# Two-layer decoder trunk: the mixer's output projection sums the squares of six first-half tiles, and the FFN loads the other two first

## The chip, the cores and the metric

The kernel runs on one core of one Trainium2 chip. The metric is the device time of one execution in microseconds (us); of several runs the median is given. The engines are called as in the profile: PE is TensorE, PEld its weight loads, DVE is VectorE, ACT is ScalarE, POOL is GpSimd, and SP is SyncE, which here issues the DMAs.

## What is computed

The reference is a decoder trunk of two layers on 1024 positions of width 1024, all in float32. Layer 0 mixes positions by a gated delta rule, layer 1 by stick-breaking attention. What matters here is the step from the mixer's output to the FFN, the same in both layers:

```
h = h + o.reshape(b_, s_, WIDTH) @ w_out          # output projection and residual
h = h + swiglu(rms_norm(h, ln_ffn[i]), ffn_w_in[i], ffn_w_out[i])

def rms_norm(x, g):
    y = x * lax.rsqrt(jnp.mean(x * x, axis=-1, keepdims=True) + EPS)
    return y * g
```

So the FFN's input needs, for each position, the mean over 1024 features of the squared result of the output projection.

## The kernel before

**Layout.** The activations lie transposed: features on partitions, positions along the free dimension. A half is 512 positions; the 1024 features are eight tiles of 128 partitions, so a half of the residual stream is eight tiles of 128x512. Matmul operands are kept as a rounded high part and a low part (hi and lo), and a product of two such operands takes three matmuls (`mm3`, line 351). One tile of a projection is therefore 8 x 3 = 24 matmuls into one PSUM bank.

**Order of the work.** The program is written as generators that a planner (`Flow`, lines 83 to 259) interleaves while the program is built. The main generator feeds the matmuls of the large products; others are spawned with a rank (lower goes first) and are resumed when the planner's clock says that what they last issued is ready. The clock is an estimate with a cost for each operation; it advances with TensorE's matmuls, and a DMA's landing is estimated with one ring of 360 GB/s (lines 202 to 204). The result is a fixed order of instructions on each engine's queue; an engine works through its queue in order and waits on semaphores where an input isn't there yet. Tiles come from pools; those with one tag share a number of buffers, and a new tile waits until a buffer of its tag is free.

**The stages round the change.** `out_first` (line 1266) makes the first half of the output projection, tile by tile. For each tile f its helper `put` loads the residual tile into a buffer (`ca` in layer 0, `xt` in layer 1), adds the projection's bank on DVE, and writes the sum to memory (`h1D`). It runs at the end of the mixer: in layer 0 from `gdn` (line 665), in layer 1 from `attention` (line 1790), where the first tiles are interleaved with the last attention steps. The mixer's pools are then closed, and `tail` (line 1302) opens those of the FFN.

`tail` makes the second half of the output projection, and its helper `put` adds each bank to a residual tile that stays in SBUF. Beside that, `load(0)` brings the first half back from `h1D` into eight tiles `u`, and for each half a generator `norm` runs at rank 1: for tile after tile `sumsq` (line 532) squares it on ACT and adds it to an accumulator `acc` on DVE (the first square goes into the accumulator directly); then `rstd` (line 544) sums the accumulator over the partitions by four matmuls with one column of ones each (tile `st`), `root` (line 552) takes the mean plus a small constant on DVE and its power -1/2 on POOL, and `normed` (line 561) spreads the result over the partitions by four matmuls and multiplies and splits the eight tiles.

When both halves are normalized, `first` and `combine` (lines 1341 and 1422) build sums and differences of the four quarter blocks on DVE, operands of a fast scheme with seven products instead of eight; the FFN's first weight pair (`f_in`, names `fg` and `fu`) is multiplied plainly with the two halves, and the rest (`f_s`) with those combinations. The weights pass through two load buffers `raw`, are split on ACT (high part) and on DVE or POOL (low part), and sit in three slots `w` and one slot `e`.

The second half of layer 0's last normalization uses a small persistent tile `r1` (line 300): it is written near the end of layer 0's tail and read at the start of attention.

## Time and profile before

| What | Before |
|---|---|
| Median of 3 runs | 2774.21 us (2772.11 to 2776.08) |
| The profiled execution's own time | 2772.17 us |
| Its span | 2770.5 us |
| PE busy in the span | 2735.0 us (99%) |
| DVE, ACT, POOL busy | 1945.8, 1325.1, 868.4 us |
| Weight loads on PE | 2273.6 us (82%) |
| Data moved by DMA | 394.85 MB, mean 143 GB/s |
| Granted TensorE clock, mean | 0.998 |

The profile is of one execution on the chip. Its page gives busy time by engine, the chain of work that ended last, and groups of instructions; the trace behind it answers for any stretch of time with busy times, with instructions in order of time (start, duration, operation, output<-inputs, count, and in brackets the idle time of the engine before it with what ended it), and with who waited for whom. Nearly all instructions pass through one helper and so carry line 64 (L64); they are told apart by the names of their tiles.

### The profile page before, as it was taken

To read this page: it belongs to the slowest core of one execution; us is meant where nothing else is said; L and a number is where in the kernel's file an instruction comes from. 1 tells how busy PE (TensorE), PEld (TensorE's weight loads), DVE (VectorE), ACT (ScalarE), POOL (GpSimd) and SP (SyncE) were. 2 spreads that over 40 slices of the span, in tenths; PEclk is the share of its full clock that TensorE was granted. 3 is DMA by queue.
4 is the path that set the end of the run, shared out by engine and by line. 5 is a ranking of instruction groups with operands and counts; after the bars stand their busy time and mean duration, and the time that the engine had idled before them with its cause. 6 is when DMAs were issued, how large, how long until landed. Compare 5 with 4: busy or idle time off the path is not lost.

```text
span 2770.5 us, 37795 instructions
## 1 busy us (share of the span) xinstructions
PE 2735.0 (99%) x13203; PEld 2273.6 (82%) x13203; DVE 1945.8 (70%) x3727; ACT 1325.1 (48%) x2701; POOL 868.4 (31%) x750
## 2 busy tenths in 40 slices
PE   9999999999999999999999999999999999999999
PEld 8788888888778888888888888888878888888787
DVE  7687888873875655477867778887696555557783
ACT  6655555543444434222335778877443333322241
POOL 0111111100166666444201222221036666634410
PEclk9999999999999999999999999999999999999999
DMA  4412222246434444577342111114514444477723
GB/s 147 144 59 77 73 77 75 74 151 234 159 107 152 164 153 148 222 313 305 124 137 100 47 58 54 54 58 149 209 61 160 150 153 142 156 288 282 279 82 125
DMA packets 165073, 394.85 MB, mean 143 GB/s; under 512 B 34001, under 2 KB 35345, under 8 KB 155409
## 3 DMA queue, kind: packets, MB, share of 16 engines
q1 hardware_dynamic: 164880, 392.43, 40.3%
q8 instruction: 104, 1.70, 0.3%
q14 instruction: 89, 0.72, 0.1%
HBM read 273.77 MB, written 118.59 MB: 142 GB/s over the span
## 4 chain that ended last, share of the span: by engine, by line
PE 88%; DVE 6%; ACT 2%; issue 2%; DMA 1%; POOL 0%; SPq 0%; ACTq 0%; POOLq 0%; DVEq 0%
PE dn L64 42%; PE mm L64 33%; PE tp L64 4%; PE z L64 3%; PE c L64 2%; PE o L64 2%; PE po L64 1%; DVE x L64 1%; PE rc L64 1%; PE st L64 1%; ACT junk L64 1%; PE r L64 1%; DVE y L64 1%; DVE v L64 0%; DVE acc L64 0%
## 5 line engine op out<-in xcount | busy, mean ns | idle before, releaser
L64 PE MATMUL mm<-x,whi 128*128 128x512 f32 x2592 | 860.1, 401 | 6.1 <-DVE x L64 5.8
L64 PE MATMUL dn<-x,whi 128*128 128x512 f32 x2032 | 628.7, 390 | 1.4 <-DVE v L64 0.9
L64 PEld LDWEIGHTS mm<-x,whi 128*128 128x128 f32 x2592 | 480.3, 189 | 94.7 <-DVE x L64 10.2
L64 PE MATMUL mm<-x,wlo 128*128 128x512 f32 x1296 | 518.7, 400 | 0.0
L64 POOL TENSOR_TENSOR wlo<-raw,whi 128x512 fp32r<-128x512 f32 x244 | 349.2, 1452 | 407.1 <-ACT whi L64 392.5
L64 ACT CAST whi<-raw 128x1024 fp32r<-128x1024 f32 x231 | 242.7, 1051 | 446.3 <-DVE raw L64 253.7
L64 PEld LDWEIGHTS dn<-x,whi 128*128 128x128 f32 x2032 | 381.4, 188 | 82.2 <-DVE x L64 2.1
L64 PE MATMUL dn<-x,wlo 128*128 128x512 f32 x1016 | 396.4, 390 | 0.0
L64 PEld LDWEIGHTS mm<-x,wlo 128*128 128x128 f32 x1296 | 244.8, 189 | 41.1 <-issue 0.3
L64 PE MATMUL dn<-hx,whi 128*128 128x512 f32 x896 | 276.9, 390 | 0.4 <-DVE hx L64 0.4
L64 PEld LDWEIGHTS dn<-x,wlo 128*128 128x128 f32 x1016 | 190.9, 188 | 39.2
L64 PEld LDWEIGHTS dn<-hx,whi 128*128 128x128 f32 x896 | 168.2, 188 | 36.3 <-DVE hx L64 1.3
L64 DVE TENSOR_TENSOR v<-v,dn 128x512 f32<-128x512 f32 x112 | 76.4, 686 | 170.4 <-PE dn L64 169.5
L64 DVE TENSOR_TENSOR tt<-u,tt 128x512 fp32r<-128x512 f32 x140 | 133.3, 952 | 80.7 <-ACT tt L64 80.7
L64 PE MATMUL dn<-hx,wlo 128*128 128x512 f32 x448 | 175.0, 391 | 3.4 <-POOL wlo L64 3.4
L64 DVE TENSOR_TENSOR wlo<-raw,whi 128x512 fp32r<-128x512 f32 x218 | 148.9, 694 | 27.2 <-ACT whi L64 26.6
L64 POOL TENSOR_TENSOR wlo<-sw,whi 128x512 fp32r<-128x512 f32 x102 | 144.8, 1437 | 0.0
L64 ACT CAST tt<-u 128x512 fp32r<-128x512 f32 x140 | 84.9, 620 | 123.0 <-DMA yD<-tt 101.6
L64 DVE TENSOR_TENSOR E<-E,dn 128x512 f32<-128x512 f32 x132 | 90.0, 684 | 70.6 <-PE dn L64 68.4
L64 PE MATMUL dn<-x,ehi 128*128 128x512 f32 x400 | 123.5, 390 | 2.3 <-ACT v L64 2.3
L64 POOL TENSOR_TENSOR rs<-ms,nhalf 128x4 f32<-128x4 f32 x11 | 12.0, 1087 | 338.7 <-DVE ms L64 338.7
L64 DVE SCALAR_TENSOR_TENSOR ca<-xe,conv,ca 128x512 f32<-128x512 f32 x144 | 106.2, 744 | 0.9 <-ACT ca L64 0.5
(381 smaller groups left out, 5092.4 us busy)
## 6 DMA issues: line engine op xcount, KB each, us to landing
yD<-tt SPq DMA_DIRECT2D x296, 256.0 KB, 2.5
x<-yD SPq DMA_DIRECT2D x58, 1024.0 KB, 11.4
raw<-f_s SPq DMA_DIRECT2D x84, 512.0 KB, 3.6
raw<-d_s SPq DMA_DIRECT2D x40, 512.0 KB, 5.1
raw<-w_in SPq DMA_DIRECT2D x33, 512.0 KB, 4.0
hx<-yD SPq DMA_DIRECT2D x16, 1024.0 KB, 13.9
x<-oD SPq DMA_DIRECT2D x26, 512.0 KB, 5.1
raw<-g_out SPq DMA_DIRECT2D x16, 512.0 KB, 4.7
```

The source lines that it names most:

```text
L64: r = issue(*args, **kw)
```

## The change

The squares of the first six of the first half's eight tiles are no longer taken in `tail` from the tiles that were loaded back. `out_first` spawns a generator `squares` for each of its first six tiles, at rank 2, as soon as the tile is added. The first square makes an accumulator, the others are added to it; behind the sixth, four matmuls with a column of ones sum it over the partitions, and DVE writes that sum times 1/1024 plus the small constant into the tile `r1`. Accumulator and squares use free buffers of the mixer's pools: tag `xe` in layer 0, `rw` in layer 1. In `tail`, `load(0)` brings tiles 6 and 7 first, the first half's `norm` squares and adds just these two, and `root` adds `r1` in place of the constant. The second half is as before. The mixer's end also waits until `r1` is marked.

```diff
-    def rstd(self, pool, acc, r):
+    def rstd(self, pool, acc, r, more=None):
...
-        yield from self.root(pool, st, r)
-
-    def root(self, pool, st, r):
+        yield from self.root(pool, st, r, more)
+
+    def root(self, pool, st, r, more=None):
         nc = self.nc
         ms = self.t(pool, "ms", (P, 4))
-        nc.vector.tensor_scalar(ms, st[:, :4], 1.0 / D, EPS, op0=ALU.mult, op1=ALU.add)
+        if more is None:
+            nc.vector.tensor_scalar(ms, st[:, :4], 1.0 / D, EPS, op0=ALU.mult, op1=ALU.add)
+        else:
+            nc.vector.scalar_tensor_tensor(ms, st[:, :4], 1.0 / D, more, op0=ALU.mult, op1=ALU.add)
...
-            yield from self.out_first(0, io["xT"], self.tmp)
-            yield lambda: all(e in flow.at for e in ("loaded00", "loaded01", ("put", 0)))
+            yield from self.out_first(0, io["xT"], self.tmp, lambda: self.g("xe", (P, HW + 3))[:, :HW])
+            yield lambda: all(e in flow.at for e in ("loaded00", "loaded01", ("put", 0), ("r1", 0)))
...
-    def out_first(self, layer, hsrc, tmp):
+    def out_first(self, layer, hsrc, tmp, room):
...
+        acc = []
+
+        def squares(xt):
+            if not acc:
+                acc.append(room())
+                yield from self.sumsq(None, acc[0], xt, True)
+            else:
+                acc.append(None)
+                yield from self.sumsq(room, acc[0], xt, False)
+            if len(acc) < NK - 2:
+                return
+            st = yield from self.bank()
+            for j in range(4):
+                self.mmul(st[:, j : j + 1], acc[0][:, j * P : (j + 1) * P], self.ones[:, :1])
+            yield
+            nc.vector.tensor_scalar(self.r1, st[:, :4], 1.0 / D, EPS, op0=ALU.mult, op1=ALU.add)
+            self.unbank(st)
+            flow.mark(("r1", layer))
...
             nc.sync.dma_start(self.h1D[layer][f][:, :HW], xt)
+            if f < NK - 2:
+                flow.spawn(squares(xt), 2)
             if f == NK - 1:
                 flow.mark(("put", layer))
...
             def load(hf):
-                for k in range(NK):
+                for k in range(NK) if hf else (6, 7, 0, 1, 2, 3, 4, 5):
...
             def norm(hf):
                 a = self.t(fp, "acc", bufs=2)
-                for k in range(NK):
+                ks = range(NK) if hf else (NK - 2, NK - 1)
+                for k in ks:
                     yield lambda: flow.done(("h1", layer, hf, k))
-                    yield from self.sumsq(lambda: self.t(fp, "tt", bufs=4), a, H1[hf, k], k == 0)
+                    yield from self.sumsq(lambda: self.t(fp, "tt", bufs=4), a, H1[hf, k], k == ks[0])
                 r = self.t(fp, "rs", (P, 4))
-                yield from self.rstd(fp, a, r)
+                yield from self.rstd(fp, a, r, None if hf else self.r1)
...
-            yield from self.out_first(1, self.hD, lambda: self.t(sp, "xt"))
-            yield lambda: all(e in flow.at for e in ("loaded10", "loaded11", ("put", 1)))
+            yield from self.out_first(1, self.hD, lambda: self.t(sp, "xt"), lambda: self.t(sp, "rw"))
+            yield lambda: all(e in flow.at for e in ("loaded10", "loaded11", ("put", 1), ("r1", 1)))
```

## The prediction

> **What bounds the kernel now.** I began with the profile page: span, busy time by engine, and the chain that ended last.

> ```profile
> span 2770.5 us, 37795 instructions
> PE 2735.0 (99%) x13203; PEld 2273.6 (82%) x13203; DVE 1945.8 (70%) x3727; ACT 1325.1 (48%) x2701; POOL 868.4 (31%) x750
> PE 88%; DVE 6%; ACT 2%; issue 2%; DMA 1%; POOL 0%; SPq 0%; ACTq 0%; POOLq 0%; DVEq 0%
> ```

> TensorE works without a pause for 2735.0 us of 2770.5, so work taken from another engine is worth only the pause of TensorE that it removes, and every matmul that is added costs its time. The table by stage shows where those pauses lie round the change (columns: PE, PEld, DVE, ACT and POOL busy with counts, granted clock, DMA share, GB/s).

> ```profile
> 644.00:690.00 46.00, 46.00 (x207) 38.12 (x206) 20.09 (x34) 12.81 (x18) 1.01 (x1) 1.00 0.85 282
> 690.00:714.00 24.00, 24.00 (x108) 19.89 (x106) 13.58 (x23) 11.52 (x17) 0.00 (x0) 1.00 0.91 317
> 714.00:719.00 5.00, 4.21 (x27) 3.51 (x26) 3.24 (x6) 2.10 (x3) 1.01 (x1) 1.00 0.53 181
> 719.00:735.00 16.00, 16.00 (x72) 13.23 (x71) 15.83 (x27) 6.94 (x11) 0.00 (x0) 1.00 0.33 113
> ...
> 755.00:785.00 30.00, 26.21 (x107) 19.25 (x107) 29.91 (x41) 14.64 (x24) 17.27 (x10) 1.00 0.06 18
> ...
> 1938.00:1984.00 46.00, 46.00 (x206) 37.92 (x205) 32.14 (x59) 24.52 (x38) 1.80 (x5) 1.00 0.44 148
> ...
> 2048.00:2078.00 30.00, 26.30 (x107) 19.30 (x106) 29.91 (x41) 14.68 (x24) 17.31 (x10) 1.00 0.06 18
> ```

> The first half's output projection ends near 688 and the second half's near 734 (layer 1 repeats the pattern about 1293 us later), by the adds that take the last tiles, and the group at 715 is where TensorE pauses:

> ```profile
> 687.91 0.69 DVE L64 TENSOR_TENSOR ca<-ca,mm 128x512 f32<-128x512 f32 x1 [3.24 <-PE mm L64]
> ...
> 715.41 1.02 PE L64 MATMUL st<-cst,acc 128*128 128x1 f32 x8 [0.79 <-DVE acc L64]
> ...
> 734.32 0.69 DVE L64 TENSOR_TENSOR E<-E,mm 128x512 f32<-128x512 f32 x1
> ```

> TensorE is full in both projections but for those 0.8 us; the clock is 1.00. Its real pauses come later, 3.8 us at 755 to 785 and 3.7 us at 2048 to 2078, where VectorE is busy 29.91 of 30 us. The waits of TensorE from 690 to 790 name the releasers:

> ```profile
> PE mm L64 <- DVE x L64: 1.4, 1, 1.4
> PE dn L64 <- ACT v L64: 1.2, 1, 1.2
> PE st L64 <- DVE acc L64: 0.8, 1, 0.8
> ```

> The third is the wait that the change touches: the matmuls that sum squares over partitions, held up by their accumulator. All that can be gained here is 0.8 + 3.8 + 3.7 = 8.3 us.

> **What the change adds to TensorE.** Each layer gets a second group of four one-column matmuls: one behind the sixth tile in the output projection, the old one still behind the seventh and eighth. In layer 1 the old group runs without a wait, so its cost can be read from TensorE's timeline (each of the four is recorded as two):

> ```profile
> 2008.18 0.39 PE L64 MATMUL mm<-x,whi 128*128 128x512 f32 x1
> 2008.41 0.95 PE L64 MATMUL st<-cst,acc 128*128 128x1 f32 x8
> ...
> 2009.77 0.63 PE L64 MATMUL mm<-x,whi 128*128 128x512 f32 x2
> ```

> Ordinary matmuls start 0.23 us apart (2008.18 to 2008.41). The two lines left out are one matmul each. From the group's start to the third matmul behind it (2009.77) are 1.36 us, of which those two take 0.46: the group costs 0.90 us. The new groups land near 679 and 1973, in stretches with no pause to hide in. Two groups: **+1.8 us**, the surest term. [...]

> **What moves off the crowded stretch.** Per layer, six squares on ScalarE and five adds on VectorE go from the second half's projection to the first's; one add disappears. Their rows, and the constant's nearest one:

> ```profile
> L64 DVE TENSOR_TENSOR acc<-acc,tt 128x512 f32<-128x512 f32 x14 | 9.4, 687 | 1.1 <-ACT tt L64 0.9
> ...
> L64 ACT ACTIVATE tt<-u 128x512 f32<-128x512 f32 x7 | 4.2, 620 | 0.0
> ...
> L64 DVE TENSOR_SCALAR ms<-st x10: 156/161/164, 716.5 to 2684.6; 128x4 f32<-128x4 f32 x10
> ```

> That is 6 x 0.62 = 3.7 us and 5 x 0.69 = 3.4 us, and one small operation of 0.16 us more. At 644 to 690 VectorE is idle for 26 us and ScalarE for 33, at 1938 to 1984 for 14 and 21; there the work is hidden, at nothing. Without that cover a square could hold up an attention step by 0.62 us, which the projection matmuls between the steps would still fill. The mean plus rest replaces a scalar operation by one with a tensor operand on 4 columns, 0.16 us or a little more, on a chain with slack. No table load comes with the squares in layer 1: attention squares 128 times beside exponentials and loads a table once from 1470 to 1930:

> ```profile
> L64 ACT ACTIVATE ajunk<-z 128x128 f32<-128x128 f32 x128 | 35.4, 277 | 12.4 <-PE z L64 9.2
> ...
> L64 ACT ACT_TABLE_LOAD x1 | 1.3, 1283 | 0.0
> ```

> The borrowed buffers, xe and rw, belong to convolutions and queries that are done by then, so nobody waits for them. A projected tile is held for its square, 0.62 us, beside its own write to memory, which takes 2.3:

> ```profile
> h1D<-ca SPq DMA_DIRECT2D x8, 256.0 KB, 2.3
> ```

> No DMA is added, and SP issues the eight loads at the same place in its queue, in another order; what is queued behind them (weights, h1D writes) keeps its place. The stage now also waits for the new constant before it ends, which is there before the last tile that it waits for anyway.

> **The wait at the remaining group.** Before, the group stood behind a serial chain of eight tiles, square and add in turn, from 703.3 to 715.3, and that length hid late loads. Now two tiles stand in front, and the planner puts the matmuls some 2 us behind the landing that it expects. ScalarE shows both layers waiting for the first tile:

> ```profile
> 699.64 0.63 ACT L64 ACTIVATE tt<-v 128x512 f32<-128x512 f32 x1
> 703.28 0.63 ACT L64 ACTIVATE acc<-u 128x512 f32<-128x512 f32 x1 [3.02 <-DMA u<-h1D]
> ...
> 1996.27 0.63 ACT L64 ACTIVATE acc<-u 128x512 f32<-128x512 f32 x1 [2.14 <-DMA u<-h1D]
> ...
> u<-h1D SPq DMA_DIRECT2D x8, 256.0 KB, 6.0
> ```

> Two squares, an add and two handovers bring the sum to 703.28 + 0.62 + 0.62 + 0.69 + about 0.3 = 705.5. If the planner expects the tile when ScalarE came free (700.3), the matmuls stand at 702.5 and TensorE waits 3.0 us; in layer 1 by the same working 2.1. If it expects it at or behind the real landing, nothing. Its model queues transfers at 360 GB/s on one ring (lines 202 to 204), near the 317 of the row for 690 to 714, and eight serial steps of some 1.45 us end at 714.4 only if the first began by about 703: so I take the lower part, 1.0 and 0.5 us. Against the 0.8 of today: **+0.7 us** (bounds -0.8 and +4.3).

> **What earlier half-0 work does later.** The first half's normalizing begins on VectorE with this multiply:

> ```profile
> 719.69 0.74 DVE L64 SCALAR_TENSOR_TENSOR u<-u,vec,st 128x512 f32<-128x512 f32 x1
> ```

> Its eight multiplies and eight subtractions fill 719 to 735; with the sum at 705.5 instead of 715.4 they move up by some ten microseconds. The second half's chain doesn't begin earlier for that: its last tile comes from TensorE at 734.3. But with a free VectorE the splits of the FFN's first weights end sooner, their buffers take the next loads sooner, and so POOL's splits may no longer collide with the second half's first subtractions:

> ```profile
> 740.69 1.41 DVE L64 SCALAR_TENSOR_TENSOR v<-v,vec,st 128x512 f32<-128x512 f32 x2 [2.47 <-PE st L64]
> 742.13 1.48 DVE L64 TENSOR_TENSOR y<-v,y 128x512 fp32r<-128x512 f32 x1
> ...
> 744.18 1.12 DVE L64 TENSOR_TENSOR y<-v,y 128x512 fp32r<-128x512 f32 x1
> ...
> 741.76 2.99 POOL L64 TENSOR_TENSOR elo<-raw,ehi 128x512 fp32r<-128x512 f32 x2
> ```

> Beside POOL the two take 1.48 and 1.12 us where a subtraction or add alone takes 0.69: 1.2 us too much, at the head of the stretch in which VectorE sets TensorE's pauses. The relief is between 0 and 1.2 us a layer; I take half, **-1.2 us** for both. What is late next there is VectorE itself, with both halves' combinations, which no part of this change shortens.

> The sum: 1.8 + 0.7 - 1.2 = +1.3 us on the profiled execution, 2772.17 (1.67 more than its span), so 2773.5. The median shown is 2774.21, 2.04 above the profiled one; the forecast for it is **2775.5 us**.

> **Rivals.** *Only the groups count:* the wait stays 0.8, nothing is relieved. For it: VectorE is full at 755 to 785 whatever happened at 719. Against: the moved work does leave slack ahead of POOL's splits. +1.8, 2776.0 us, within the measurement.

> *Slower: loads later than planned.* The two-tile chain no longer covers the landing, and TensorE, whose queue is in order, sits at the first-half group with the whole second-half projection queued behind it. For: ScalarE waits 3.02 and 2.14 us for exactly these loads, DMA share 0.91. Against: the planner models the backlog. Price: waits of 3.0 and 2.1 instead of 0.8, +4.3, with the groups +6.1: 2780.3 us. It decides from the point where the waits exceed some 4.5 us together and the relief stays out.

> *Faster: VectorE runs ahead.* If the freed 3 to 4 us of VectorE per layer reach the stretch at 755 and 2048, all pauses go: -8.3 + 1.8 = -6.5, 2767.7 us. For: VectorE is what TensorE waits for there. Against: it was idle for 2.47 us just before 740.69, waiting for the second half, so its backlog doesn't come from the first half.

> *It doesn't do what it says:* the remaining chain could stay as late as before, if the planner served the two tiles behind the second half's. Then only the groups count, the first rival's time.

> **How the numbers follow.** A measurement of this kernel can tell about 0.2%, 5.5 us, from no change. My forecast has 0.60, the groups alone 0.20, late loads 0.13, VectorE ahead 0.07. The first two lie within 0.2%, so same 0.80; slower 0.13, faster 0.07. The range: lowest with the wait gone and full relief, 1.8 - 0.8 - 2.4 = -1.4, and 2 us below for the spread of the runs shown (2772.11 to 2776.08), 2770.8; highest the late loads, 2780.3, with little on top: 2770.8 to 2781.0. It leaves out the faster rival and some of the slower one.

> **What would show it.** Right: eight more one-column matmuls in each layer, from xe near 679 and from rw near 1973, with no pause around them; squares of ca between 650 and 680 and of xt in layer 1; the first-half u multiplies starting near 709 instead of 719.7; VectorE well below its 15.83 us in 719 to 735; the 755 to 785 stretch still full on VectorE with 2.6 to 3.8 us of TensorE pauses. Wrong: a wait of over 2 us at the remaining group, pauses near 679 or 1973, the u multiplies no earlier than before, or TensorE without pauses at 755 to 785. A changed order far behind, in attention or the FFN's products, with pauses of several us would also defeat it, since the planner orders everything anew.

## The result and the profile after

| What | Before | After |
|---|---|---|
| Median of 4 runs | 2773.66 us (2772.11 to 2776.08) | 2787.67 us (2786.88 to 2796.97) |
| After by before, 95% interval | | 1.0054 (1.0042 to 1.0066) |
| The profiled execution's own time | 2772.17 us | 2796.97 us |
| Its span | 2770.5 us | 2795.3 us |
| PE busy | 2735.0 us | 2750.1 us |
| Mean granted TensorE clock | 0.998 | 0.992 |

The change makes the kernel slower: the ratio says 0.54%, and the medians lie 14.0 us apart. The ratios here and below were measured with their intervals; they are not quotients of the medians beside them, which come out up to 0.09% away. The profiled execution is the longest of the four; the others took 2786.88 to 2788.38 us at a mean clock of 0.995. Its trace is read against its own 2796.97 us, and part of what it shows is its own, as is said at the first pause below. One execution of a kernel further down, that with all four holds, ran at a mean clock of 0.556 and took 4577.75 us; its ratio leaves it out, its median of 2774.59 us counts it.

The page of the changed kernel, the lines that answer to those of before:

```profile
span 2795.3 us, 37808 instructions
PE 2750.1 (98%) x13219; PEld 2284.8 (82%) x13219; DVE 1943.4 (70%) x3727; ACT 1325.7 (47%) x2701; POOL 862.4 (31%) x750
PE 86%; DVE 6%; ACT 3%; issue 2%; DMA 1%; POOL 1%; SPq 0%; POOLq 0%; DVEq 0%; ACTq 0%
```

TensorE has the 16 new matmul records and is busy 15.1 us longer; it also has 9.7 us more of idle span. The 16 records are two groups of the prediction's 0.90 us; the rest of the busy time goes with the lower mean clock, 0.992 against 0.998, and the table by stage shows where (same columns as in the prediction):

```profile
680.00:690.00 10.00, 8.39 (x34) 6.74 (x34) 4.63 (x8) 1.68 (x2) 0.00 (x0) 0.83 0.57 200
690.00:705.00 15.00, 15.00 (x68) 12.43 (x67) 6.17 (x10) 5.27 (x6) 0.00 (x0) 1.00 0.75 249
705.00:720.00 15.00, 12.38 (x49) 10.27 (x48) 6.32 (x12) 4.25 (x7) 1.01 (x1) 0.77 0.72 277
744.00:780.00 36.00, 34.29 (x157) 27.79 (x156) 30.79 (x47) 17.67 (x29) 12.64 (x8) 1.00 0.11 37
780.00:804.00 24.00, 20.50 (x75) 15.79 (x75) 17.62 (x23) 7.70 (x11) 12.85 (x9) 0.86 0.15 56
...
2010.00:2025.00 15.00, 13.10 (x53) 10.88 (x52) 6.74 (x12) 4.07 (x6) 1.01 (x1) 0.77 0.64 244
2085.00:2105.00 20.00, 16.48 (x64) 12.58 (x64) 15.04 (x19) 7.21 (x11) 12.85 (x9) 0.91 0.19 66
```

Five stretches have a granted clock below 1.00 (a mix of 1.00 and of 0.50, called half clock from here on), and each of them also has a pause (length less PE busy). One minus the clock, times the length, is the clock lost: 10 x 0.17 = 1.7 us, 15 x 0.23 = 3.4, 24 x 0.14 = 3.4, 3.4 and 1.8, together 13.7 us. Before, the same stages ran at 1.00. TensorE's timeline names the pauses:

```profile
682.72 1.23 PE L64 MATMUL tp<-cst,xe 128*128 128x1 f32 x8 [1.61 <-DVE xe L64]
...
710.31 1.50 PE L64 MATMUL st<-cst,acc 128*128 128x1 f32 x8 [2.62 <-DVE acc L64]
...
786.57 0.51 PE L64 MATMUL dn<-x,whi 128*128 128x512 f32 x1 [1.12 <-DVE x L64]
...
789.92 0.80 PE L64 MATMUL dn<-x,whi 128*128 128x512 f32 x1 [2.38 <-DVE x L64]
...
2014.19 0.47 PE L64 MATMUL st<-cst,acc 128*128 128x1 f32 x3 [1.90 <-DVE acc L64]
```

The first is the new group, the second and the last are the remaining groups of the two layers, the others are FFN products that wait for VectorE.

The first pause comes from the timing of this execution, not from the order of the instructions. Three kernels of the experiments (the remaining group held, the mixer's half alone, the sums late) issue the same instructions in the same order on every engine up to 700 us, and in none of their profiles does TensorE wait here. With the sums late, the group stands so:

```profile
680.29 0.95 PE L64 MATMUL tp<-cst,xe 128*128 128x1 f32 x8
```

In the profiled execution the sixth add came late, at 680.08 behind 3.99 us of idle VectorE. The pause of 1.6 us and a mean clock lower by 0.003 (an estimate of some 8 us, which holds the 1.7 us behind the pause) are about the 9.6 us by which this execution is longer than the other three.

Behind the remaining groups stands the load. ScalarE's timeline (idle time and releaser in brackets):

```profile
708.14 0.63 ACT L64 ACTIVATE acc<-u 128x512 f32<-128x512 f32 x1 [2.94 <-DMA u<-h1D]
...
2011.99 0.63 ACT L64 ACTIVATE acc<-u 128x512 f32<-128x512 f32 x1 [2.57 <-DMA u<-h1D]
```

These waits were there before, 3.02 and 2.14 us; now TensorE stands behind them. That tiles 6 and 7 are loaded first is not what makes the load late: from the first issue to ScalarE's first square it is 708.1 - 701.5 = 6.6 us in layer 0, before 703.3 - 696.6 = 6.7, and 6.3 us in layer 1 in both kernels. The last add of the second half gives the sum. After, then before (its first-layer time is in the prediction):

```profile
744.17 0.68 DVE L64 TENSOR_TENSOR E<-E,mm 128x512 f32<-128x512 f32 x1
...
2047.83 0.69 DVE L64 TENSOR_TENSOR E<-E,mm 128x512 f32<-128x512 f32 x1 [0.65 <-PE mm L64]
```

```profile
2027.26 0.69 DVE L64 TENSOR_TENSOR E<-E,mm 128x512 f32<-128x512 f32 x1
```

In layer 0 it is 744.17 - 734.32 = 9.85 us late: the new group 0.9, its pause 1.6, lost clock 1.7, the remaining group's 2.62 - 0.79 = 1.8 and lost clock 3.4 make 9.4. From there to the first table load behind the layer the lag grows to 13.9 (1493.25 against 1479.33), in the stretch 780 to 804. In layer 1 it grows by 6.7 to 20.57 (a group 0.9, the pause 1.9, lost clock 3.4), and at 2085 to 2105 to 24.8 us, where it stays to the end.

### The profile page after: what moved, and what is told of

It is laid out like the page before. It is cut to its first block, busy times and chain, and to the rows that moved or that the text cites. A ratio compares the mean times of both kernels' runs of the same rounds, so it can differ in the third digit from the quotient of the medians.

```text
span 2795.3 us, 37808 instructions
## 1 busy us (share of the span) xinstructions
PE 2750.1 (98%) x13219; PEld 2284.8 (82%) x13219; DVE 1943.4 (70%) x3727; ACT 1325.7 (47%) x2701; POOL 862.4 (31%) x750
## 4 chain that ended last, share of the span: by engine, by line
PE 86%; DVE 6%; ACT 3%; issue 2%; DMA 1%; POOL 1%; SPq 0%; POOLq 0%; DVEq 0%; ACTq 0%
PE dn L64 41%; PE mm L64 31%; PE tp L64 4%; PE z L64 3%; PE c L64 2%; PE o L64 2%; DVE x L64 1%; PE po L64 1%; PE rc L64 1%; PE r L64 1%; DVE acc L64 1%; PE st L64 1%; ACT L64 1%; ACT junk L64 1%; DMA u<-h1D 0%
## 5 line engine op out<-in xcount | busy, mean ns | idle before, releaser
L64 PE MATMUL mm<-x,whi 128*128 128x512 f32 x2592 | 860.5, 401 | 3.6 <-DVE x L64 3.4
L64 PE MATMUL dn<-x,whi 128*128 128x512 f32 x2032 | 628.9, 390 | 7.0 <-DVE x L64 7.0
L64 PEld LDWEIGHTS mm<-x,whi 128*128 128x128 f32 x2592 | 481.3, 189 | 91.7 <-DVE x L64 6.1
L64 PE MATMUL mm<-x,wlo 128*128 128x512 f32 x1296 | 519.6, 401 | 0.0
L64 POOL TENSOR_TENSOR wlo<-raw,whi 128x512 fp32r<-128x512 f32 x244 | 346.7, 1442 | 485.2 <-ACT whi L64 457.2
L64 PEld LDWEIGHTS dn<-x,whi 128*128 128x128 f32 x2032 | 381.5, 188 | 88.1 <-DVE x L64 8.8
L64 ACT CAST whi<-raw 128x1024 fp32r<-128x1024 f32 x231 | 242.6, 1051 | 441.3 <-DVE raw L64 241.5
L64 PE MATMUL dn<-x,wlo 128*128 128x512 f32 x1016 | 396.1, 390 | 0.0
L64 PEld LDWEIGHTS mm<-x,wlo 128*128 128x128 f32 x1296 | 245.5, 189 | 41.7 <-issue 0.3
L64 PE MATMUL dn<-hx,whi 128*128 128x512 f32 x896 | 277.0, 390 | 0.0
L64 PEld LDWEIGHTS dn<-x,wlo 128*128 128x128 f32 x1016 | 191.2, 188 | 39.4
L64 PEld LDWEIGHTS dn<-hx,whi 128*128 128x128 f32 x896 | 168.7, 188 | 35.6 <-ACT whi L64 0.4
L64 DVE TENSOR_TENSOR v<-v,dn 128x512 f32<-128x512 f32 x112 | 76.4, 686 | 169.8 <-PE dn L64 168.6
L64 DVE TENSOR_TENSOR tt<-u,tt 128x512 fp32r<-128x512 f32 x140 | 133.1, 951 | 81.0 <-ACT tt L64 81.0
L64 PE MATMUL dn<-hx,wlo 128*128 128x512 f32 x448 | 175.5, 392 | 3.4 <-POOL wlo L64 3.4
L64 DVE TENSOR_TENSOR wlo<-raw,whi 128x512 fp32r<-128x512 f32 x218 | 148.9, 693 | 25.0 <-ACT whi L64 24.4
L64 DVE TENSOR_TENSOR E<-E,dn 128x512 f32<-128x512 f32 x132 | 89.9, 684 | 80.6 <-PE dn L64 78.3
L64 POOL TENSOR_TENSOR wlo<-sw,whi 128x512 fp32r<-128x512 f32 x102 | 145.7, 1446 | 0.0
L64 ACT CAST tt<-u 128x512 fp32r<-128x512 f32 x140 | 84.8, 619 | 123.7 <-DMA yD<-tt 95.1
L64 PE MATMUL dn<-x,ehi 128*128 128x512 f32 x400 | 123.4, 390 | 1.6 <-ACT v L64 1.6
L64 DVE SCALAR_TENSOR_TENSOR ca<-xe,conv,ca 128x512 f32<-128x512 f32 x144 | 106.3, 744 | 0.9 <-ACT ca L64 0.4
L64 PEld LDWEIGHTS dn<-hx,wlo 128*128 128x128 f32 x448 | 84.4, 188 | 22.1 <-POOL wlo L64 4.7
## 6 DMA issues: line engine op xcount, KB each, us to landing
yD<-tt SPq DMA_DIRECT2D x296, 256.0 KB, 2.8
hx<-yD SPq DMA_DIRECT2D x16, 1024.0 KB, 13.9
```

The source lines that it names most:

```text
L64: r = issue(*args, **kw)
```

## The experiments

Two theories at first. A: pauses at the one-column groups, and half clock behind each, make the time. B: the planner's new order further back makes it, near 786 and 2090 us. A hold is a `yield` of so many us of the planner's clock.

**Holding the groups back.** The first kernel holds the remaining group, the second the new one, the third both:

```diff
                 r = self.t(fp, "rs", (P, 4))
+                if hf == 0:
+                    yield 4.0
                 yield from self.rstd(fp, a, r, None if hf else self.r1)
```

```diff
             if len(acc) < NK - 2:
                 return
+            yield 4.0
             st = yield from self.bank()
```

> The changed kernel, but the first half's normalizing waits 4 planned us before the four matmuls of its remaining group, so that TensorE gets other products first. Theory A (pauses and clock): the changed kernel's 14 us are pauses of TensorE at one-column groups and the half clock that follows each of them; the waits of 2.62 us in layer 0 and 1.9 us in layer 1 at this group go, with some 1.5 to 2 us of lost clock behind each, so about -8 us: 2779 to 2781 us. Theory B (order): the time is made further back, by the new order of splits beside VectorE at 785 and 2090 us, and the group's pauses only come earlier what would be waited for there: 2785 to 2788 us.

> The changed kernel, but the new group behind the sixth tile waits 4 planned us before its matmuls. Theory A: the wait of 1.61 us at 682.7 and the half clock from 683.8 to 686.9 go, about 1.5 us more; nothing in layer 1, where this group had no wait: about -3, 2784.5 us. Theory B: 2786 to 2788 us.

> Both groups held back by 4 planned us. Theory A: -8 and -3 add up to about -11: 2776 to 2778 us, what is left over the kernel before being the two groups (1.8 us) and the waits near 786 and 2090 us. Theory B: 2785 us or more, with the waits near 786 and 2090 as large as in the changed kernel.

Measured against the kernel before on the same chip (2775.83 us): remaining group held 2780.78 us, ratio 1.0016 (1.0007 to 1.0025); new group held 2790.8 us, 1.0060 (1.0047 to 1.0074); both held 2780.46 us, 1.0016 (1.0007 to 1.0025). Holding the remaining group takes most of the loss away, as A says. Holding the new one takes nothing: the pause there came from one execution's timing, and the remaining groups waited 2.92 and 2.50 us. With both held, TensorE's waits from 640 to 860 us begin with another place:

```profile
PE st L64 <- POOL rs L64: 2.1, 1, 2.1
PE mm L64 <- DVE x L64: 1.3, 1, 1.3
```

That is the next four matmuls, which spread the result and now wait for GpSimd's power (2.1 us here, 0.7 in layer 1). But the pauses near 786 us were gone as well, which A had left in. They were gone with the remaining group alone held, too, so these two kernels changed more than the group's waits.

**A ladder of pauses.** The kernel before with 36 groups or chains put into the FFN's products, in one execution:

```diff
+    def pause(self, w, n):
+        st = yield from self.bank()
+        if w:
+            self.mmul(st[:, :8], self.ident, self.ones[:, :8])
+            self.nc.vector.tensor_copy(self.p0, st[:, :8])
...
+                self.nc.gpsimd.tensor_tensor(self.p1[:, :c], src[:, :c], self.nhalf[:, :c], op=ALU.pow)
...
+            self.mmul(st[:, :1], self.ident, self.p1[:, c - 1 : c])
+        for j in range(n):
+            self.mmul(st[:, j % 4 : j % 4 + 1], self.ident, self.ones[:, :1])
```

> The kernel before with pauses put into the FFN's dense products by hand, the result's numbers untouched by them: in layer 0 eighteen chains TensorE - VectorE - GpSimd - TensorE of nine lengths, each twice (the GpSimd power has 1 to 14 columns, by the row of 1.01 us for four columns some 0.5 to 2.8 us, with handovers pauses of about 1 to 3.5 us), ordinary matmuls behind them; in layer 1 groups of 4, 8, 16 and 32 one-column matmuls without a pause, and pauses of five lengths with a group of four behind, each twice. Theory A: up to about 1.4 us the granted clock stays at 1.00 behind a pause, from about 1.6 us on the next 3 to 4 us run at half clock, so that a pause of 2 us costs about 4; a group of one-column matmuls behind a pause acts like more pause. Rival: the drop does not follow the length of the pause (it comes at random, or only behind one-column groups), and pauses of 2 to 3 us with ordinary matmuls behind leave the clock at 1.00.

Three pauses from TensorE's timeline, the third with a group of four calls (eight records) behind it, and a group of sixteen calls with no pause:

```profile
1052.53 0.38 PE L68 MATMUL st<-p,cst 128*128 128x1 f32 x2 [1.41 <-POOL p L68]
...
1074.11 0.38 PE L68 MATMUL st<-p,cst 128*128 128x1 f32 x2 [1.87 <-POOL p L68]
...
2209.14 4.84 PE L68 MATMUL st<-cst 128*128 128x1 f32 x32
...
2291.22 0.38 PE L68 MATMUL st<-p,cst 128*128 128x1 f32 x2 [1.28 <-POOL p L68]
2291.47 1.03 PE L68 MATMUL st<-cst 128*128 128x1 f32 x8
```

And the table by stage just behind each of the four:

```profile
1053.53:1055.00 1.47, 1.47 (x8) 1.17 (x7) 0.17 (x1) 0.63 (x1) 1.47 (x3) 1.00 0.32 42
...
1075.00:1077.00 2.00, 2.00 (x6) 1.54 (x5) 1.27 (x3) 1.25 (x2) 2.00 (x3) 0.50 0.27 82
...
2214.00:2217.00 3.00, 3.00 (x8) 2.32 (x9) 2.25 (x4) 1.25 (x2) 1.28 (x1) 0.50 0.11 45
...
2294.00:2296.00 2.00, 2.00 (x6) 1.58 (x5) 1.37 (x1) 0.53 (x2) 1.28 (x1) 0.50 0.85 312
```

In the ladder the clock is 1.00 or 0.50, and the loss behind a pause, added up in steps of 1 us, was 0, 1.7 or 3.4 us and nothing between. With ordinary matmuls behind: pauses of 1.12 to 1.57 us lost clock in 1 of 5, of 1.71 to 2.50 in 6 of 9, of 2.97 to 3.90 in 4 of 4. With a group of four behind: pauses of 1.12 to 2.52 us in 9 of 10. A group alone lost none with four or eight calls (0 of 4), and with sixteen or thirty-two each time (4 of 4). So in this execution half clock followed pauses, the longer ones more often, and the groups of sixteen and thirty-two brought it without a pause: what A says is borne out, though not with a sharp edge. The stretches of half clock behind the chains and groups all start on one grid of 3.41 us: the first four, at 845.97, 869.87, 914.24 and 938.13, are 7, 13 and 7 steps apart. One step at half clock loses 1.7 us, the smallest loss above. Why only one of the two pauses of 1.57 us with ordinary matmuls behind lost clock, no run shows.

**One half of the change at a time.** Rival C puts the cost into the mixer's half. Three edits: the tail's half alone (of the kernel before), the mixer's half alone (of the changed kernel) and the groups alone (of the kernel before):

```diff
-                for k in range(NK):
+                for k in range(NK) if hf else (6, 7, 0, 1, 2, 3, 4, 5):
...
+                ks = range(NK) if hf else (NK - 2, NK - 1)
+                for k in ks:
```

```diff
-                for k in range(NK) if hf else (6, 7, 0, 1, 2, 3, 4, 5):
+                for k in range(NK):
...
-                ks = range(NK) if hf else (NK - 2, NK - 1)
+                ks = range(NK)
...
-                yield from self.rstd(fp, a, r, None if hf else self.r1)
+                yield from self.rstd(fp, a, r, None)
```

```diff
+        def group():
+            st = yield from self.bank()
+            for j in range(4):
+                self.mmul(st[:, j : j + 1], self.ident, self.ones[:, :1])
...
+            if f == NK - 3:
+                flow.spawn(group(), 2)
```

The fourth kernel is that with both holds, and one hold more, behind `rstd`:

```diff
                 yield from self.rstd(fp, a, r, None if hf else self.r1)
+                if hf == 0:
+                    yield 3.0
```

> The kernel before with the tail's half of the change alone: tiles 6 and 7 are loaded first and only these two are squared and summed; the squares of the six others are left out, so the first half's mean lacks them. No second group, no work added in the mixer's output projection. Theory A (pauses and clock): the exposed group pauses as in the changed kernel, 2.6 us in layer 0 against 0.8 and 1.9 us in layer 1, with 1.7 or 3.4 us of lost clock behind each, and the pauses near 786 and 2090 with theirs: some 8 to 11 us of the changed kernel's excess are here, 2783 to 2787 us. Rival C (the mixer's half costs): the squares and the new group make most of it, and this kernel is within 3 us of the kernel before.

> The changed kernel with the mixer's half alone: six squares of each layer are summed there with the new group and its constant, but the tail loads in the old order and squares all eight tiles again, and does not use the sum from the mixer. Theory A: the two groups of 0.9 us and, in layer 0, the pause of 1.6 us and 1.7 us of lost clock behind it: +2 to +5, 2778 to 2781 us. Rival C: most of the changed kernel's excess, 2784 us or more.

> The kernel before with one more group of four one-column matmuls per layer behind the sixth tile's add, of constants, so that it waits for nothing, with its small operation on VectorE and the same wait at the mixer's end; no squares. By the prediction's step: 0.90 us a group, +1.8, 2777.6 us, not to be told from the kernel before. Otherwise, if the groups themselves upset the planner's order: +4 or more.

> The changed kernel with both groups held back by 4 planned us, and the four matmuls that spread the result over the partitions by another 3, since in the kernel with two holds TensorE waits 2.1 and 0.7 us there for the GpSimd power. Theory A: these 2.8 us go, and what is left over the kernel before is the two groups less its own pause of 0.8: 2776 to 2778 us. Theory B (order): 2780 us or more.

Kernel before 2776.51 us. Tail's half: 2787.69 us, ratio 1.0046 (1.0033 to 1.0059). Mixer's half: 2777.21 us, 1.0004 (0.9995 to 1.0013). Groups alone: 2777.04 us, 1.0006 (0.9997 to 1.0015). So C falls: nearly all of the loss comes with the tail's half and its shortened chain; what the squares and the groups cost is too small to be told from nothing. TensorE's waits in the kernel with the tail's half alone, from 640 to 860 us:

```profile
PE dn L64 <- DVE x L64: 3.5, 2, 2.4
PE st L64 <- DVE acc L64: 3.3, 2, 2.6
```

They are the waits of the changed kernel, without any square added to the mixer's output projection. The kernel with three holds took 2782.9 us, 1.0031 (1.0019 to 1.0042), and here A falls as the whole story. Its waits in the same stretch:

```profile
PE dn L64 <- DVE x L64: 3.5, 2, 2.4
PE st L64 <- DVE acc L64: 1.4, 1, 1.4
PE dn L64 <- ACT v L64: 0.7, 1, 0.7
```

TensorE waits at neither first-half group (the 1.4 us are the second half's), and the 3.5 us near 786 are back. They have a cause of their own. They are not a net price: the kernel before waits 3.8 us at 755 to 785, at most 1.4 at a time; here all waits from 640 to 860 come to 6.7 us, the largest is 2.4, and the stretch from 770 to 800 ran at a clock of 0.89, 3.3 us lost.

**The early splits.** GpSimd's timeline before and after shows a difference that goes with those waits in every kernel so far:

```profile
738.29 1.01 POOL L64 TENSOR_TENSOR rs<-ms,nhalf 128x4 f32<-128x4 f32 x1 [20.58 <-DVE ms L64]
739.27 2.53 POOL L64 TENSOR_TENSOR wlo<-raw,whi 128x512 fp32r<-128x512 f32 x2
741.76 2.99 POOL L64 TENSOR_TENSOR elo<-raw,ehi 128x512 fp32r<-128x512 f32 x2
```

```profile
744.83 2.97 POOL L64 TENSOR_TENSOR wlo<-raw,whi 128x512 fp32r<-128x512 f32 x2 [31.73 <-ACT whi L64]
747.75 1.29 POOL L64 TENSOR_TENSOR elo<-raw,ehi 128x512 fp32r<-128x512 f32 x1
749.00 1.01 POOL L64 TENSOR_TENSOR rs<-ms,nhalf 128x4 f32<-128x4 f32 x1
```

Before, the second half's power goes first and the splits of the first combined weight pair (`f_s`) follow. After, the planner puts the pair's four sums ahead of the second half's last add; the splits then stand ahead of the power and beside the last square's add, as VectorE's timeline of the changed kernel shows:

```profile
741.51 0.69 DVE L64 TENSOR_TENSOR sw<-raw,raw 128x512 f32<-128x512 f32 x1 [0.85 <-DMA raw<-f_s]
...
744.17 0.68 DVE L64 TENSOR_TENSOR E<-E,mm 128x512 f32<-128x512 f32 x1
745.61 1.05 DVE L64 TENSOR_TENSOR acc<-acc,tt 128x512 f32<-128x512 f32 x1 [0.76 <-ACT tt L64]
747.88 0.16 DVE L64 TENSOR_SCALAR ms<-st 128x4 f32<-128x4 f32 x1 [1.21 <-PE st L64]
751.25 1.41 DVE L64 SCALAR_TENSOR_TENSOR v<-v,vec,st 128x512 f32<-128x512 f32 x2 [3.21 <-PE st L64]
```

From the last add to the first multiply are 751.25 - 744.17 = 7.1 us against 740.69 - 734.32 = 6.4 before. That isn't yet the price: the two subtractions that follow now run alone and take 0.69 and 0.68 us instead of 1.48 and 1.12, and the second ends 10.5 us behind the last add, before 11.0. What TensorE waits for near 786 are two later operations, `x<-E,x`. VectorE's timeline before, then after:

```profile
772.29 0.68 DVE L64 TENSOR_TENSOR x<-E,x 128x512 fp32r<-128x512 f32 x1
...
776.99 1.78 DVE L64 TENSOR_TENSOR x<-E,x 128x512 fp32r<-128x512 f32 x1
```

```profile
784.75 1.76 DVE L64 TENSOR_TENSOR x<-E,x 128x512 fp32r<-128x512 f32 x1
...
788.12 1.75 DVE L64 TENSOR_TENSOR x<-E,x 128x512 fp32r<-128x512 f32 x1
```

Counted from the last add, they start at 40.6 and 43.9 us against 38.0 and 42.7, and now both stand beside GpSimd's splits of a later pair. So it is in all four kernels with the 3.5 us (the changed one, the new group held, three holds, the tail's half), in both layers; in every other kernel up to here the first takes 0.68 us and starts at 38.0. Why the planner moves them when the sums come early, no run shows.

Theory D makes this a cost of its own; E makes the pauses near 786 follow from those at the first half's group. Two kernels hold the sums back, one on the changed kernel and one on that with three holds; the third brings them forward in the kernel before:

```diff
                         yield lambda: self.fp is not None
+                        if key[0] == "fs" and key[2] == 0:
+                            yield lambda: ("h1", key[1], 1, NK - 1) in flow.at
                         yield from sums(key[:-1], (raws[i - 1][0], raw))
```

```diff
-                yield lambda: len(raws) > i and flow.now >= raws[i][1] + 2.0 * (key[0] == "fs")
+                yield lambda: len(raws) > i and flow.now >= raws[i][1] + (2.0 if key[0] == "fs" and key[2] else -1.0) * (key[0] == "fs")
```

> The changed kernel, but the sums of the FFN's first combined weight pair are held on VectorE until the second half's last tile has been added, as they stood in the kernel before; so GpSimd's splits of that pair again stand behind its power for the second half. Theory D (the early splits are a cost of their own): in the changed kernel these splits sit ahead of the power and of the subtractions that TensorE needs near 786 and 2090 us, and the pauses of 3.5 us in each layer (largest 2.4) with the lost clock of 3.4 and 1.7 us behind them come from that. They go, and the pattern of the kernel before comes back (VectorE x 1.3, ScalarE v 1.2, VectorE v 0.5, y 0.4 us); the waits of 2.6 and 1.9 us at the first half's group stay with their lost clock: 2780 to 2784 us. Theory E (all of it follows from the waits at the first half's group): the pauses of 3.5 us stay, 2787 us.

> The kernel with three holds (2782.9 us), and the sums of the first combined weight pair held back as well. Theory D: no wait at the first half's groups, and the pattern of the kernel before near 786 and 2090 us, so what is left over the kernel before is the two groups, 1.8 us, less its own pause of 0.8: 2776 to 2779 us where the kernel before has 2776. Theory E: the hold of the sums changes nothing, 2782 to 2784 us.

> The kernel before, where only the first combined weight pair counts as ready 3 us earlier for the planner, so that its sums stand ahead of the second half's last add and GpSimd's splits ahead of its power, as in the changed kernel; squares, loads and groups are those of the kernel before. Theory D: the pauses of 3.5 us a layer near 780 and 2080 us appear here too, with 1.7 to 3.4 us of lost clock each: +4 to +8, 2780 to 2784 us, without any wait added at the first half's group. Theory E: within 2 us of the kernel before.

Kernel before 2776.14 us. Sums late in the changed kernel: 2785.14 us, 1.0041 (1.0027 to 1.0054). All four holds: 2774.59 us, 0.9997 (0.9988 to 1.0006). Sums early in the kernel before: 2782.6 us, 1.0028 (1.0017 to 1.0040). E falls. With the sums late, TensorE's waits read:

```profile
PE st L64 <- DVE acc L64: 3.2, 1, 3.2
PE mm L64 <- DVE x L64: 1.4, 1, 1.4
```

The 3.5 us are gone and the old pattern is back, as D says; but the waits at the remaining groups grew to 3.25 and 2.30 us, with 1.7 us of lost clock behind each, so the time lies 1.1 us above the range that D gave. With all four holds nothing is left of either (the first two lines of the same view):

```profile
PE mm L64 <- DVE x L64: 1.3, 1, 1.3
PE dn L64 <- ACT v L64: 1.2, 1, 1.2
```

Sums early cost 0.28% with no pause added at the first half's group beyond 1.33 us. The time is D's, the shape not quite: in layer 0 the wait moved to the second half's group (2.18 us), only in layer 1 do the `dn` products wait for x (4.1 us, the largest 1.7), and no clock was lost behind them. TensorE's idle time grew by 3.5 and 4.0 us in the two layers (8.1 against 4.6 us at 640 to 860, 7.7 against 3.7 at 1940 to 2180), and that is the 0.28%. Here the price is paid at the head: from the last add to the end of the second subtraction are 12.2 us, before 11.0.

So both causes are shown, each with the other taken away: the early order alone 1.0031 (1.0019 to 1.0042), waits at the remaining groups alone 1.0041. Whether they add up can't be told: the ratios do not (0.31 and 0.41% against 0.54%), the medians nearly do (6.4 and 9.0 us against 14.0), and each is uncertain by some 0.12%. Two things stay open. The edits move the pair's sums on VectorE and its splits on GpSimd together, so no run tells which of the two moves costs. And how many pauses lose clock in an execution without a profile, no run shows; the mean clocks of 0.998 and 0.995 give an estimate of (0.998 - 0.995) x 2785 = 8 of the 14 us, give or take 3 for the rounding to thousandths.

## Why the prediction was wrong, point by point

**Groups: right, as far as it can be measured.** 0.90 us each, +1.8, is 1.0006; groups alone measured 1.0006 (0.9997 to 1.0015), which doesn't exclude nothing.

**Squares hidden: right.** The mixer's half measured 1.0004 (0.9995 to 1.0013). The pause of 1.61 us at the new group contradicts "with no pause around them", but it came from one execution's timing: three kernels with the same instructions up to there had none.

**The failed step: the wait at the remaining group.** The prediction took 1.0 and 0.5 us out of 3.0 and 2.1, +0.7 in all. Measured were 2.62 and 1.90, near the upper ends, so +3.7. The reason given for the lower part, when the old chain of eight steps ended, said nothing of when the planner would place the matmuls behind two. What came is the case that the prediction worked out first, matmuls placed as if the tile were there when ScalarE comes free: it came free at 705.20, the tile let it start 2.94 us later, and TensorE waited 2.62 (2.57 and 1.90 us in layer 1).

**The missing term: the clock.** The sum charged a pause its own length. The prediction's row at 755 to 785 showed pauses at a clock of 1.00, and the largest there was 1.4 us; those at the groups are longer and have one-column matmuls behind them. Their lost clock, 3.4 us in each layer of the profiled execution, is more than the pauses; with the sums late it was 1.7 us behind each. The profile of before did hold a sign that no step of the prediction read: 1925 to 1936 us, with 1.9 us of pauses, ran at a clock of 0.84.

**The relief: there, but outweighed.** -1.2 us was put down for both layers. The subtractions did get rid of GpSimd, and by the full 1.2 us in each (0.69 and 0.68 us, not 1.48 and 1.12). What came with it is the early order: the pair's splits ahead of GpSimd's power, its sums ahead of the second half's last add, and `x<-E,x` beside GpSimd near 786 and 2090. That alone cost 0.3%. The prediction named "a changed order far behind", with pauses, among the signs of being wrong, but gave it no price and no chance.

**The slower rival** had the place and the waits right (3.0 and 2.1 us), and came to 2780.3 us without lost clock and early splits; that is why the range ended at 2781.0. Its chance of 0.13 was too low for two rows that showed ScalarE waiting for just these loads. The u multiplies, due near 709, began at 716.75. Of these 7.8 us, 4.9 are the lag with which the first tile was there (708.14 against 703.28), and some 2 the longer way from the group to the multiply, much of it at half clock (6.4 us against 4.3).

## What to carry to other kernels

A long chain of small steps ahead of a group can be what hides a late load (in layer 0 TensorE waited 0.79 us behind eight tiles and 2.62 behind two); shorten it only together with a later place for the group, and price the wait by what the trace shows of the load, not by what a planner expects. A pause of TensorE is to be priced with the half clock that may follow: in the ladder 1.7 or 3.4 us were lost behind 10 of 13 pauses of 1.71 to 3.90 us, behind 1 of 5 of 1.12 to 1.57, and with four one-column calls behind in 9 of 10 of 1.12 to 2.52. Work taken off an engine can let other work be planned sooner: look which queue that work then heads, and what stands beside what some 40 us later.
